# RG-LRU gates of a hybrid layer: two 64-channel blocks on the two halves of the TensorE array's rows

## The chip, the core and the metric

The kernel runs on one core of a Trainium2 chip. The core has five engines that work side by side, each through its own queue in order: PE (TensorE, matmul; its weight loads are shown apart as PEld), DVE (VectorE), ACT (ScalarE), POOL (GpSimd) and SP (SyncE, which issues most transfers). Operands lie in SBUF and matmul results in PSUM, which has eight banks; both memories have 128 partitions, and the partitions of a matmul's operands are the rows of PE's array. The metric is the device time of one execution in microseconds (us).

## The reference

One layer of a streaming encoder: an RMS norm, one combined input projection, differential attention beside a gated linear recurrence (RG-LRU), one output projection and a final norm. The input has 1024 tokens of width 1024, with 16 meta tokens ahead of them (T = 1040). The part that the change concerns is the two gates of the recurrence, each a block-diagonal product with eight blocks of 64 x 64:

```python
def rg_lru(x, w_r, b_r, w_i, b_i, lru_L):
    B, T, C = x.shape                                # C = 512
    xb = x.reshape(B, T, N_LRU_BLOCKS, LRU_BLOCK)    # 8 blocks of 64 channels
    r = jax.nn.sigmoid(jnp.einsum('btnc,ncd->btnd', xb, w_r).reshape(B, T, C) + b_r)
    i = jax.nn.sigmoid(jnp.einsum('btnc,ncd->btnd', xb, w_i).reshape(B, T, C) + b_i)
    log_a = -LRU_C * r * jax.nn.softplus(-lru_L)
    a = jnp.exp(log_a)
    mult = jnp.sqrt(-jnp.expm1(2.0 * log_a))
    mult = mult.at[:, 0].set(1.0)
    b = mult * (i * x)
    ...                                              # h[t] = a[t] * h[t-1] + b[t]
```

## The kernel before

Channels lie on partitions and tokens along the free dimension, so the 512 recurrent channels are four tiles (b = 0 to 3) of 128 partitions x 1040 tokens, two 64-channel blocks in each. A tile's tokens are cut into three thirds of 264, 264 and 512 columns (COLS, line 34), each of which fits a PSUM bank. Every fp32 product is made of three matmuls on a split of its operands into a high and a low part: high x high, high x low, low x high.

**Gates before.** The weights of both gates lie as full 128 x 128 matrices with two 64 x 64 blocks on the diagonal and zeros elsewhere (wg, line 1291; split into wgh and wgl by gate_weights, line 662). For each tile, gate and third, `gate` (line 530) takes one bank, makes three matmuls on all 128 rows, and ACT reads the bank once with a sigmoid on 128 partitions. That is 24 thirds, 72 matmuls and 24 sigmoids.

**Where they run.** The input projection runs in groups of 32 steps by `run_group` (line 685): K, Q, GA (the attention's gate path), GL (the recurrence's gate path), each with four blocks of eight steps over the contraction. A step is six matmuls of 512 columns (in K six of 264 and three of 512). After each step `tick` (line 156) takes items from a background list `bg`, in which conv, split, gates, decay and scan of the four tiles stand in a fixed order (lines 702 to 723). An item has a cost that is charged to a credit, may carry a function that says when its inputs are ready, and an item without a function ends the tick. The times for this come from a model of the engines (`Clock`, line 38) at the time the program is built; what results is one fixed order for each engine. While K runs, the gates of tile 0 use the bank O (`gate_bank`, line 515), later gates use the pool M of three banks, which also serves other work.

**What follows a gate.** On ACT: tanh of gate 0 (named `gate` in the views, by sp4), then `a` (one plus it); DVE then takes five reciprocals of `a` and multiplies gate 1 with xc (`lru_decay`). Then `lru_scan`: a square root on ACT (with a table load ahead), a multiply on DVE, `a` again on ACT, the product with gate 1 and the scan on DVE.

**Beside it on the same two engines.** `split_steps` (line 220) prepares the next group's weights, one contraction step at a time: a copy on ACT (w<-wraw), a subtraction on DVE (w<-wraw,w), and PE needs both in that step of the next group's first block. `qk_evac` (line 617) and `ga_evac` (line 747) take finished blocks out of PSUM: qk on DVE, f16h on ACT, f16l on DVE; for GA a sigmoid gsig on ACT and a product gsig on DVE, two each for a block.

Of the kernel before, what the change touches and what calls it, by code (L numbers as in the profile page):

```python
# [9 lines left out]
F32R = mybir.dt.float32r  # L10
F16 = mybir.dt.float16
BF16 = mybir.dt.bfloat16
AF = mybir.ActivationFunctionType
# [3 lines left out]
P = 128  # L17
NM = 16
S = 1024
T = NM + S  # L20
# [5 lines left out]
NB = 4  # L26
# [72 lines left out]
def hybrid_layer_kernel(ctx: ExitStack, tc: tile.TileContext, xT, x, meta, w6, nwT,  # L99
                        par, wg, lamv, subw, w_out, fnw, cosT, sinT, ident, sel, bmask, out):  # L100
    nc = tc.nc
    clock = Clock()
    V, A, G, PE = (clock.engine(k, e) for k, e in zip(("V", "A", "G", "PE"),
                                                      (nc.vector, nc.scalar, nc.gpsimd, nc.tensor)))
# [14 lines left out]
    def slot(tag, shape, dt=F32, name=None):  # L119
        return big.tile(shape, dt, tag=tag, bufs=BUFS[tag], name=name or tag)  # L120

    def cst(shape, dt=F32, name=None):
        return const.tile(shape, dt, name=name)

    def bank(shape, dt=F32, name="psm"):
        ps = psM.tile(shape, dt, tag="M", name=name)
        clock.ring("M", 3, ps)
        return ps
# [44 lines left out]
    def later(*items):  # L173
        bg.extend(items)
# [140 lines left out]
    for k in range(KC - 2):  # L315
# [3 lines left out]
        if k == 1:  # L319
            pr = cst([P, NB, 8], name="pr")  # L320
# [41 lines left out]
        fetch_w(G_K, k)  # L362


    wgr = slot("V", [P, NB, 2, P], name="wgr")
    dma(wgr, wg)
    cosR = slot("K", [P, T], name="cosR")
    dma(cosR, cosT)
# [14 lines left out]
    def row_of_rstd():  # L383

        dg = slot("raw", [P, 4, P], name="dg"), slot("raw", [P, 4, P], name="dg")
        dm = cst([NM, NM], name="dgm")
        for h in range(2):
            V.tensor_tensor(dg[h], idf.unsqueeze(1).to_broadcast([P, 4, P]),
                            rstd[:, 4 * h:4 * h + 4].unsqueeze(2).to_broadcast([P, 4, P]), op=OP.mult)
        V.tensor_scalar(dm, idf[0:NM, 0:NM], rstd[0:NM, NT:NT + 1], None, op0=OP.mult)  # L390
        yield
        ps, pm = two_banks(), bank([P, NM], name="psx")
        for h in range(2):
            PE.matmul(ps[:, h * 512:(h + 1) * 512], ones, dg[h].rearrange("p t q -> p (t q)"), start=True, stop=True)
            A.copy(Rb[:, NM + h * 512:NM + (h + 1) * 512], ps[:, h * 512:(h + 1) * 512])
        PE.matmul(pm, ones[0:NM, :], dm, start=True, stop=True)
        A.copy(Rb[:, 0:NM], pm)
        yield
# [28 lines left out]
    rows = row_of_rstd()  # L427
# [58 lines left out]
    L = [{} for _ in range(NB)]  # L486
# [26 lines left out]
    in_k = []  # L513

    def gate_bank():
        if in_k:
            ps = psO.tile([P, 512], F32, tag="O", name="psg")
            clock.ring("O", 1, ps)
            return ps
        return bank([P, 512], name="psg")  # L520


    def lru_gates(b):


        def gate_ready(j, h):
            return max(clock.ready(L[b]["ch"], L[b]["cl"]) if j + h == 0 else 0.0,
                       clock.free("O", 1) if in_k else clock.free("M", 3))

        def gate(j, h):  # L530
            ch, cl = L[b]["ch"], L[b]["cl"]
            if h == 0:
                L[b]["ti"[j]] = slot("work", [P, T], name=f"gate{j}")
            r, bias = L[b]["ti"[j]], pr[:, b, 5 + j:6 + j]
            ps = gate_bank()
            s = COLS[h]
            ps = ps[:, 0:s.stop - s.start]
            PE.matmul(ps, wgh[:, b, j, :], ch[:, s], start=True, stop=False)
            PE.matmul(ps, wgh[:, b, j, :], cl[:, s], start=False, stop=False)
            PE.matmul(ps, wgl[:, b, j, :], ch[:, s], start=False, stop=True)  # L540
            A.activation(r[:, s], ps, AF.Sigmoid, bias=bias)

        def tanh():
            t = L[b]["t"]
            A.activation(t, t, AF.Tanh, scale=sp4[:, b:b + 1])
            a = L[b]["a"] = slot("work", [P, T], name="a")
            A.activation(a, t, AF.Identity, bias=1.0)

        for j in range(2):
            for h in range(3):  # L550
                later((0, lambda j=j, h=h: gate(j, h), lambda j=j, h=h: gate_ready(j, h)), (0, None))
        later((0, tanh))

    def lru_decay(b):
# [106 lines left out]

    def gate_weights():
        nonlocal wgh, wgl
        wgh = slot("V", [P, NB, 2, P], F32R, name="wgh")
        wgl = slot("V", [P, NB, 2, P], F32R, name="wgl")
        A.copy(wgh, wgr)
        V.tensor_tensor(wgl, wgr, wgh.bitcast(F32), op=OP.subtract)
        V.tensor_copy(idh, idf)
# [31 lines left out]

    wgh = wgl = None
    later((0, tables), (1.15, gate_weights))
    lru_conv(0)
    lru_split(0)
    lru_conv(1)
    lru_gates(0)
    later((0.6, masks), (0, meta_operand))
    lru_split(1)
    lru_conv(2)
    lru_decay(0)  # L710
    lru_gates(1)
    lru_split(2)
    lru_conv(3)
    later(*lru_scan(0))
    lru_decay(1)
    lru_gates(2)
    lru_split(3)
    later(*lru_scan(1))
# [558 lines left out]
def _layout(i):  # L1277
    f = np.float32
    a = {k: np.asarray(v) for k, v in i.items()}
    x = a["x"][0]  # L1280
    meta = a["meta_tokens"]
    w = a["w_in"][0]

    perm = [m * 64 + half * 8 + j for half in range(2) for m in range(NMAP) for j in range(8)]
    perm += [m * 64 + 16 * b + j for b in range(1, 4) for m in range(NMAP) for j in range(16)]
    perm = np.array(perm)
    cols = [w[:, 2048:2560], w[:, 2560:3072], w[:, 0:512][:, perm], w[:, 512:1024][:, perm],
            w[:, 1536:2048], w[:, 1024:1536]]
    par = np.concatenate([a["conv_w"][0], a["conv_b"], a["b_rgate"], a["b_igate"], a["lru_L"]], 0)
    par = par.reshape(8, NB, P).transpose(2, 1, 0)  # L1290
    wg = np.zeros((P, NB, 2, P), f)
    for n in range(8):
        b, o = n // 2, (n % 2) * 64
        wg[o:o + 64, b, 0, o:o + 64] = a["w_rgate"][0, n]
        wg[o:o + 64, b, 1, o:o + 64] = a["w_igate"][0, n]

    inv = np.power(np.float64(500000.0), -np.arange(0, 16, 2) / 16).astype(f)
    ang = (np.arange(T, dtype=f)[:, None] * inv[None, :]).astype(np.float64)
    row = np.arange(P) % 8
    cosT = np.cos(ang).astype(f).T[row]  # L1300
    sinT = np.sin(ang).astype(f).T[row]
    sinT = np.concatenate([sinT[:64], -sinT[64:]], 0)
    r = np.arange(P)
    sel = (np.arange(32)[:, None] % NM == r[None, :] % NM).astype(f)
    bmask = ((r[:, None] % 64) // NM == np.arange(512)[None, :] // P).astype(f)
    return dict(
        xT=np.concatenate([meta, x], 0).T, x=x, meta=meta,
        w6=np.stack(cols), nwT=a["norm_w"][0].reshape(KC, P).T, par=par, wg=wg,
        lamv=np.concatenate([a["lambda_q1"], a["lambda_q2"], a["lambda_k1"], a["lambda_k2"]], 0),
        subw=a["subln_w"][0].reshape(P, 1), w_out=a["w_out"][0], fnw=a["final_norm_w"],  # L1310
        cosT=cosT, sinT=sinT, ident=np.eye(P, dtype=f), sel=sel, bmask=bmask)
# [19 lines left out]
```

## Time and profile before

| | |
|---|---|
| median of three runs | 486.93 us (486.28 to 487.14) |
| the profiled execution | 486.57 us, of which the profile's span is 484.8 us |
| matmuls of the gates (psg) | 72, from 69.7 to 182.2 us of the span |
| sigmoids of the gates | 24, from 71.0 to 182.4 us |

In rows of the timeline the columns are start and length in us, engine, line, operation, written tile <- read tiles, for PE and PEld the rows * columns of the array that are used, the shape, and the count; in brackets the idle time of the engine ahead of the row and what ended it. In rows for one tile the three numbers are the shortest, median and longest duration in ns, and then the first and last start. In rows of windows come the window, its length, the busy time of PE, PEld, DVE, ACT and POOL with the number of instructions, PE's granted clock, the busy share of the DMA engines and GB/s. All engine operations of this kernel go through one helper and so have its line, L77; one goes by the tiles' names.

### The profile page before, as it was taken

How to read it: one execution, taken by the hardware profiler on the slowest of the kernel's cores; microseconds unless marked ns; L12 is line 12 of the kernel's file. 1: busy time of each engine (PE TensorE's matmuls, PEld its weight loads, DVE VectorE, ACT ScalarE, POOL GpSimd, SP SyncE). 2: the span in 40 equal slices, each digit the busy share in tenths (PEclk: the TensorE clock that was granted, in tenths of full speed). 3: DMA queues.
4: the chain of work that ended last, by engine and by line, in shares of the span. 5: the costliest groups of instructions: out<-in, count | busy, mean ns of one | idle time of the engine just before them, and what ended most of it. 6: DMA issues, size and time to landing. Idle time of an engine off the chain costs nothing.

```text
span 484.8 us, 7748 instructions
## 1 busy us (share of the span) xinstructions
PE 466.2 (96%) x2844; PEld 375.4 (77%) x2844; DVE 364.3 (75%) x610; ACT 303.3 (63%) x592; POOL 126.1 (26%) x171
## 2 busy tenths in 40 slices
PE   6999999999999999999999999999988999999894
PEld 5996989988888888888877577777766778877783
DVE  5756987496799576974574477789999989898443
ACT  5687532663626838441583367698787877797733
POOL 0102202201010000000001044185142425365772
PEclk9999999999999999999999999999999999999998
DMA  7993221344023115239445124953943576315523
GB/s 243 394 398 124 89 89 31 80 121 120 23 65 88 44 43 174 87 124 346 141 139 187 45 61 138 265 172 91 275 110 91 131 193 153 121 32 197 195 88 130
DMA packets 50150, 68.33 MB, mean 141 GB/s; under 512 B 21008, under 2 KB 30128, under 8 KB 50112
## 3 DMA queue, kind: packets, MB, share of 16 engines
q1 hardware_dynamic: 38240, 55.21, 34.6%
q0 software_dynamic: 11872, 12.63, 10.7%
q8 instruction: 22, 0.36, 0.3%
q14 instruction: 16, 0.13, 0.1%
HBM read 48.91 MB, written 18.91 MB: 140 GB/s over the span
## 4 chain that ended last, share of the span: by engine, by line
PE 87%; DVE 5%; ACT 3%; issue 2%; DMA 1%; POOL 0%; POOLq 0%; ACTq 0%; SPq 0%
PE pss L77 42%; PE psv L77 9%; PE psol L77 7%; PE psoa L77 7%; PE ps L77 6%; PE psx L77 5%; PE O L77 4%; DVE e L77 3%; PE psg L77 2%; PE pt L77 2%; DMA res<-res_d 1%; DVE w L77 1%; PE psmr L77 1%; PE pa L77 1%; ACT wT L77 1%
## 5 line engine op out<-in xcount | busy, mean ns | idle before, releaser
L77 PE MATMUL pss<-xs,w 128*128 128x512 f32 (+1 forms) x720 | 142.4, 345 | 4.3 <-ACT xs L77 4.3
L77 PEld LDWEIGHTS pss<-xs,w 128*128 128x128 f32 x720 | 120.4, 190 | 24.5 <-ACT xs L77 4.3
L77 ACT ACTIVATE e<-e,mx 128x528 f32<-128x528 f32 (+7 forms) x64 | 50.5, 790 | 27.4 <-DVE mx L77 26.1
L77 PE MATMUL psv<-w,xs 128*128 128x512 f32 x192 | 48.4, 402 | 0.2 <-DVE v L77 0.2
L77 DVE CUSTOM_DVE_ANT_0 e<-pss,mask,nesc 128x528 f32<-128x528 f32 (+6 forms) x56 | 42.6, 761 | 7.7 <-PE pss L77 6.5
L77 PE MATMUL pss<-w,xs 128*128 128x512 f32 x192 | 46.0, 394 | 0.0
L77 PE MATMUL psol<-woh,lr 128*128 128x512 f32 x128 | 42.8, 415 | 1.9 <-ACT wT L77 1.9
L77 DVE TENSOR_TENSOR w<-wraw,w 128x512 fp32r<-128x512 f32 (+2 forms) x49 | 31.7, 669 | 16.2 <-ACT w L77 16.0
L77 PE MATMUL pss<-kst,qt 128*128 128x512 f16 (+3 forms) x208 | 42.6, 318 | 0.7 <-DVE mx L77 0.7
L77 PEld LDWEIGHTS psv<-w,xs 128*128 128x128 f32 x192 | 35.3, 188 | 10.0 <-issue 0.8
L77 PEld LDWEIGHTS pss<-w,xs 128*128 128x128 f32 x192 | 35.7, 188 | 7.9
L77 PE MATMUL psoa<-woh,at 128*128 128x512 f32 (+1 forms) x136 | 41.6, 389 | 0.2 <-ACT psoa L77 0.2
L77 ACT COPY wT<-pt 128x1024 f16<-128x1024 f16 (+5 forms) x48 | 37.6, 784 | 1.0 <-PE pt L77 0.8
L77 DVE SCALAR_TENSOR_TENSOR e<-e,mx 128x528 f32<-128x528 f32 (+7 forms) x32 | 35.0, 1095 | 1.1
L77 ACT ACTIVATE w<-wraw 128x512 fp32r<-128x512 f32 x47 | 28.5, 619 | 9.7 <-DMA wraw<-in_w_dram 9.2
L77 PE MATMUL ps<-xs,w 128*128 128x512 f32 x120 | 34.4, 394 | 0.0
L77 PEld LDWEIGHTS <-wT 128*128 128x128 f16 x432 | 25.6, 98 | 6.6 <-issue 2.7
L77 PE MATMUL O<-v,wT 128*128 128x128 f16 x432 | 29.4, 219 | 1.3 <-ACT wT L77 1.3
L77 DVE TENSOR_TENSOR w<-e,w 128x528 f16<-128x528 f32 (+7 forms) x32 | 28.9, 904 | 0.9
L77 PEld LDWEIGHTS psol<-woh,lr 128*128 128x128 f32 x128 | 22.9, 188 | 8.6 <-ACT wT L77 3.2
L77 DVE RECIPROCAL a<-a 128x208 f32<-128x208 f32 x20 | 27.8, 1423 | 0.0
L77 PEld LDWEIGHTS psoa<-woh,at 128*128 128x128 f32 x136 | 24.1, 188 | 4.5 <-ACT psoa L77 0.4
(197 smaller groups left out, 838.4 us busy)
## 6 DMA issues: line engine op xcount, KB each, us to landing
wraw<-in_w_dram SPq DMA_DIRECT2D x47, 256.0 KB, 3.9
xt<-in_x_dram SPq DMA_DIRECT2D x8, 512.0 KB, 7.0
woraw<-in_w_out_dram SPq DMA_DIRECT2D x8, 512.0 KB, 3.5
xres<-in_x_dram SPq DMA_DIRECT2D x8, 512.0 KB, 4.9
lr<-lru_d POOLq DMA_DIRECT2D x8, 512.0 KB, 5.1
res_d<-xres SPq DMA_DIRECT2D x8, 512.0 KB, 3.1
res<-res_d SPq DMA_DIRECT2D x8, 512.0 KB, 4.4
out_dram<-res SPq DMA_DIRECT2D x7, 512.0 KB, 2.9
```

The costliest lines, as they stand in the source:

```text
L77: return f(*a, **k)
```

## The change

Both gates of one 64-channel block now lie side by side in one 64 x 128 matrix. The two blocks of a tile have the two halves of the array's rows: rows 0 to 63 for the first, 64 to 127 for the second. The weights shrink to half (128 x 4 x 128). For a tile and a third, `gates` takes two banks, one for each block, and makes three pairs of matmuls on 64 rows each, alternating between the halves. Bank m then holds the gates of block m: for block 0 gate 0 on partitions 0 to 63 and gate 1 on 64 to 127, for block 1 the other way round. Four sigmoids of 64 partitions, two on each bank, carry them to the two gate tiles. There are again 72 matmuls with the same numbers of columns, in 12 groups instead of 24, and 48 sigmoids instead of 24. The list `bg` has three gate items for a tile instead of six, and an item waits for two banks.

```diff
-    wgr = slot("V", [P, NB, 2, P], name="wgr")
+    wgr = slot("V", [P, NB, P], name="wgr")
...
-        def gate_ready(j, h):
-            return max(clock.ready(L[b]["ch"], L[b]["cl"]) if j + h == 0 else 0.0,
-                       clock.free("O", 1) if in_k else clock.free("M", 3))
+        def gate_ready(h):
+            return max(clock.ready(L[b]["ch"], L[b]["cl"]) if h == 0 else 0.0,
+                       max(clock.free("O", 1), clock.free("M", 3)) if in_k else clock.free("M", 2))
 
-        def gate(j, h):
+        def gates(h):
             ch, cl = L[b]["ch"], L[b]["cl"]
             if h == 0:
-                L[b]["ti"[j]] = slot("work", [P, T], name=f"gate{j}")
-            r, bias = L[b]["ti"[j]], pr[:, b, 5 + j:6 + j]
-            ps = gate_bank()
+                for j in range(2):
+                    L[b]["ti"[j]] = slot("work", [P, T], name=f"gate{j}")
             s = COLS[h]
-            ps = ps[:, 0:s.stop - s.start]
-            PE.matmul(ps, wgh[:, b, j, :], ch[:, s], start=True, stop=False)
-            PE.matmul(ps, wgh[:, b, j, :], cl[:, s], start=False, stop=False)
-            PE.matmul(ps, wgl[:, b, j, :], ch[:, s], start=False, stop=True)
-            A.activation(r[:, s], ps, AF.Sigmoid, bias=bias)
+            n = s.stop - s.start
+            banks = gate_bank(), bank([P, 512], name="psg")
+            lohi = slice(0, 64), slice(64, P)
+            for w, x, first, last in ((wgh, ch, True, False), (wgh, cl, False, False), (wgl, ch, False, True)):
+                for m, rows in enumerate(lohi):
+                    PE.matmul(banks[m][:, 0:n], w[rows, b, :], x[rows, s], start=first, stop=last)
+            for m, rows in enumerate(lohi):
+                for c, to in enumerate(lohi):
+                    j = m ^ c
+                    A.activation(L[b]["ti"[j]][rows, s], banks[m][to, 0:n], AF.Sigmoid, bias=pr[rows, b, 5 + j:6 + j])
...
-        for j in range(2):
-            for h in range(3):
-                later((0, lambda j=j, h=h: gate(j, h), lambda j=j, h=h: gate_ready(j, h)), (0, None))
+        for h in range(3):
+            later((0, lambda h=h: gates(h), lambda h=h: gate_ready(h)), (0, None))
...
-        wgh = slot("V", [P, NB, 2, P], F32R, name="wgh")
-        wgl = slot("V", [P, NB, 2, P], F32R, name="wgl")
+        wgh = slot("V", [P, NB, P], F32R, name="wgh")
+        wgl = slot("V", [P, NB, P], F32R, name="wgl")
...
-        wg[o:o + 64, b, 0, o:o + 64] = a["w_rgate"][0, n]
-        wg[o:o + 64, b, 1, o:o + 64] = a["w_igate"][0, n]
+        wg[o:o + 64, b, o:o + 64] = a["w_rgate"][0, n]
+        wg[o:o + 64, b, 64 - o:P - o] = a["w_igate"][0, n]
```

The fixed order of the engines moves with it between 69 and about 212 us of the span; POOL and SP keep their order, and so do all engines in the attention that follows. Three places show it. Numbers that the program gives to buffers differ between the two.

PE, the last gates (tile 3) in the middle of GA, before: pss<-w,xs are GA's matmuls, pss<-xs,w are those of GL.

```order
L77 MATMUL psg<-xch,wgh 128x264
L77 MATMUL psg<-xcl,wgh 128x264
L77 MATMUL psg<-xch,wgl 128x264
L77 MATMUL pss<-w,xs 128x512 x6
L77 MATMUL psg<-xch,wgh 128x512
L77 MATMUL psg<-xcl,wgh 128x512
L77 MATMUL psg<-xch,wgl 128x512
L77 MATMUL pss<-w,xs 128x512 x90
L77 MATMUL pss<-xs,w 128x512 x192
```

The same place now:

```order
L77 MATMUL psg<-xch,wgh 128x264 x2
L77 MATMUL psg<-xcl,wgh 128x264 x2
L77 MATMUL psg<-xch,wgl 128x264 x2
L77 MATMUL pss<-w,xs 128x512 x12
L77 MATMUL psg<-xch,wgh 128x512 x2
L77 MATMUL psg<-xcl,wgh 128x512 x2
L77 MATMUL psg<-xch,wgl 128x512 x2
L77 MATMUL pss<-w,xs 128x512 x78
L77 MATMUL pss<-xs,w 128x512 x192
```

The last gates stand 78 matmuls ahead of GL instead of 90.

ACT, the end of Q, before: f16h are evacuations of Q, w the weights of GA, the gates those of tile 2 (1472 is gate 0, 1515 gate 1).

```order
L77 ACTIVATE f16h<-qk,sc 128x1024
L77 ACTIVATE w<-wraw 128x512 x3
L77 ACT_TABLE_LOAD
L77 ACTIVATE gate_1472<-psg,pr 128x264
L77 ACTIVATE w<-wraw 128x512
L77 ACTIVATE gate_1472<-psg,pr 128x264
L77 ACTIVATE w<-wraw 128x512
L77 ACTIVATE gate_1472<-psg,pr 128x512
L77 ACTIVATE w<-wraw 128x512
L77 ACTIVATE gate_1515<-psg,pr 128x264
L77 ACTIVATE f16h<-qk,sc 128x1024
```

And now (1502 is gate 0, 1503 gate 1):

```order
L77 ACTIVATE f16h<-qk,sc 128x1024
L77 ACTIVATE w<-wraw 128x512 x5
L77 ACT_TABLE_LOAD
L77 ACTIVATE gate_1502<-psg,pr 64x264
L77 ACTIVATE gate_1503<-psg,pr 64x264 x2
L77 ACTIVATE gate_1502<-psg,pr 64x264
L77 ACTIVATE w<-wraw 128x512
L77 ACTIVATE f16h<-qk,sc 128x1024
L77 ACTIVATE gate_1502<-psg,pr 64x264
L77 ACTIVATE gate_1503<-psg,pr 64x264 x2
L77 ACTIVATE gate_1502<-psg,pr 64x264
```

Five weight copies instead of three stand between f16h and the first sigmoid of tile 2. PE's matmuls for the second third of this tile use, on their second bank, the bank that the first two of these sigmoids give back.

DVE, from tile 2's scan to the weights of GL, before: the reciprocals are those of tile 3, w the weights of GL's eight steps, gsig the products of GA, 1675 and 1641 tile 3's gate 1 and gate 0.

```order
L77 SCALAR_TENSOR_TENSOR gate_1515<-a,gate_1472 128x1040
L77 RECIPROCAL a<-a 128x208 x4
L77 TENSOR_TENSOR w<-wraw,w 128x512
L77 RECIPROCAL a<-a 128x208
L77 SCALAR_TENSOR_TENSOR gsig<-pss,rstd,gsig 128x512 x2
L77 TENSOR_TENSOR gate_1675<-gate_1675,xc 128x1040
L77 TENSOR_TENSOR w<-wraw,w 128x512
L77 SCALAR_TENSOR_TENSOR gate_1641<-gate_1641,a 128x1040
L77 TENSOR_TENSOR w<-wraw,w 128x512
L77 TENSOR_TENSOR gate_1641<-gate_1641,gate_1675 128x1039
L77 COPY gate_1641<-gate_1675 128x1
L77 TENSOR_TENSOR w<-wraw,w 128x512 x2
```

And now (1684 and 1683 are tile 3's gate 1 and gate 0):

```order
L77 SCALAR_TENSOR_TENSOR gate_1503<-a,gate_1502 128x1040
L77 RECIPROCAL a<-a 128x208 x3
L77 TENSOR_TENSOR w<-wraw,w 128x512
L77 SCALAR_TENSOR_TENSOR gsig<-pss,rstd,gsig 128x512 x2
L77 RECIPROCAL a<-a 128x208
L77 TENSOR_TENSOR w<-wraw,w 128x512
L77 RECIPROCAL a<-a 128x208
L77 TENSOR_TENSOR w<-wraw,w 128x512
L77 TENSOR_TENSOR gate_1684<-gate_1684,xc 128x1040
L77 TENSOR_TENSOR w<-wraw,w 128x512 x2
L77 SCALAR_TENSOR_TENSOR gate_1683<-gate_1683,a 128x1040
L77 TENSOR_TENSOR w<-wraw,w 128x512 x2
```

Two reciprocals that stood ahead of the product gsig of GA's third block now stand behind it, between the weights of GL's first three steps; tile 3's scan (gate 1 from `a` and gate 0) moves from between the weights of steps 4 and 5 to behind the last of them.

More of the change, by code (lines that the diff above doesn't have):

```diff
@@ L1290, in _layout @@
     par = par.reshape(8, NB, P).transpose(2, 1, 0)
-    wg = np.zeros((P, NB, 2, P), f)
+    wg = np.zeros((P, NB, P), f)
     for n in range(8):
         b, o = n // 2, (n % 2) * 64
-        wg[o:o + 64, b, 0, o:o + 64] = a["w_rgate"][0, n]
-        wg[o:o + 64, b, 1, o:o + 64] = a["w_igate"][0, n]
+        wg[o:o + 64, b, o:o + 64] = a["w_rgate"][0, n]
+        wg[o:o + 64, b, 64 - o:P - o] = a["w_igate"][0, n]
     inv = np.power(np.float64(500000.0), -np.arange(0, 16, 2) / 16).astype(f)
```

## The prediction

> **What bounds the kernel now.** First the page: spans, engines and the chain that ended last.
>
> ```profile
> span 484.8 us, 7748 instructions
> PE 466.2 (96%) x2844; PEld 375.4 (77%) x2844; DVE 364.3 (75%) x610; ACT 303.3 (63%) x592; POOL 126.1 (26%) x171
> PE 87%; DVE 5%; ACT 3%; issue 2%; DMA 1%; POOL 0%; POOLq 0%; ACTq 0%; SPq 0%
> ```
>
> Then the view by windows for the stages in which gates run (K from 57, Q from 105.5, the gate-path projection GA from 154.6, GL from 203), and the row of the gate weights' copy.
>
> ```profile
> 57.00:68.00 11.00, 11.00 (x71) 9.96 (x70) 10.31 (x13) 4.13 (x8) 0.00 (x0) 1.00 0.34 122
> 68.00:183.00 115.00, 115.00 (x591) 97.63 (x591) 89.65 (x95) 62.22 (x90) 15.20 (x38) 1.00 0.24 65
> 183.00:248.00 65.00, 65.00 (x285) 52.48 (x284) 44.30 (x50) 34.21 (x52) 3.31 (x6) 1.00 0.58 185
> L77 ACT CAST wgh<-wgr x1: 1034/1034/1034, 58.4 to 58.4; 128x1024 fp32r<-128x1024 f32 x1
> ```
>
> PE (the number after the length) is never idle there; PEld, DVE and ACT follow. So what PE gains or loses between 57 and 248 us goes straight to the end, and the other engines count only where PE comes to wait for them. The halved gate weights (half of a 1.03 us copy on ACT, half of a subtraction on DVE, half of one transfer) lie beside this full PE; I cost them at nothing, and without that cover they would be worth half a microsecond.
>
> **The matmuls.** The timeline of PE shows the pace.
>
> ```profile
> 112.45 0.28 PE L77 MATMUL psg<-xch,wgh 128*128 128x264 f32 x1
> ...
> 112.81 1.55 PE L77 MATMUL pss<-xs,w 128*128 128x512 f32 x6
> ...
> 115.94 0.39 PE L77 MATMUL psg<-xch,wgh 128*128 128x512 f32 x1
> ...
> 116.63 1.55 PE L77 MATMUL pss<-xs,w 128*128 128x512 f32 x6
> ```
>
> Three gate matmuls of 264 columns take 112.81 - 112.45 = 0.36 us, 0.12 each; three of 512 take 0.69, 0.23 each. Before, one third of one tile costs six: 0.72 or 1.38 us. There are eight such groups of 264 and four of 512. After, a group is three pairs, one matmul on rows 0-63 and one on rows 64-127, into different banks. No row of this trace shows two halves side by side: a pair costs between one matmul (0.12, 0.23) and two. I take one, because the two share neither array rows nor a bank, so neither has to wait for what the other holds; I keep two for the range. The Trainium skill ("TensorEngine Tiling (Array Packing)", Key Properties) says that different tiles load weights and multiply in parallel; no run here shows it yet.
>
> **The switches.** Going from full-height matmuls to fewer rows and back is shown, with 16 and 32 rows.
>
> ```profile
> 45.71 0.59 PE L77 MATMUL pss<-dg,ones 128*128 128x512 f32 x1
> 46.23 0.29 PEld L77 LDWEIGHTS psx<-dgm,ones 16*128 16x128 f32 x2 [0.76 <-DVE sp L77]
> 277.78 0.18 PEld L77 LDWEIGHTS psvm<-mrows,sl 32*128 32x128 f32 x1
> 277.78 0.29 PEld L77 LDWEIGHTS psvm<-mrows,sl 32*128 32x128 f32 x2
> 278.31 0.59 PE L77 MATMUL psvm<-mrows,sl 32*128 32x512 f32 x1
> 278.83 0.53 PEld L77 LDWEIGHTS psv<-w,xs 128*128 128x128 f32 x3 [0.76 <-issue]
> ```
>
> Two loads follow each other by 0.29 - 0.18 = 0.11. So the first psvm matmul streams from 277.89, and the second from 278.31: a stream takes 0.42. The second ends at 278.73, but the full-height load behind it, which otherwise runs under the matmul ahead, starts only at 278.83. A switch back thus costs 0.10 of waiting and 0.11 of uncovered load, some 0.20 us. The way in is the same: 45.71 + 0.42 = 46.13, load at 46.23. Each of the twelve groups switches twice, 0.40 us. Bounds for 64 rows: a load alone (0.11) and this 0.20; I take 0.20, the measured one.
>
> Sum on PE: a group of 264 becomes 0.40 + 0.36 = 0.76 instead of 0.72, a group of 512 becomes 0.40 + 0.69 = 1.09 instead of 1.38. 8 x 0.04 - 4 x 0.29 = **-0.8 us**. The switches eat nearly all of the halving.
>
> **The sigmoids.** The same columns are read twice, 64 partitions at a time, with 48 instructions for 24.
>
> ```profile
> L77 ACT ACTIVATE gate<-psg,pr x24: 462/482/692, 71.0 to 182.4; 128x264 f32<-128x264 f32 x16, 128x512 f32<-128x512 f32 x8
> L77 DVE TENSOR_TENSOR ropet<-ps,sinR x2: 674/680/686, 76.6 to 78.0; 64x512 f32<-64x512 f32 x2
> ```
>
> No ACT row has 64 partitions; half the time and all of it are the bounds, and I take all of it: durations here go with columns, and DVE's ropet piece of 64x512 takes 0.68 us, like the last 128x512 row quoted below (0.67). Back to back they start 0.1 closer than their length: 0.38 and 0.59. ACT gains 13 us of work over 115 us. Mostly that is hidden, as ACT is busy for 62 of those 115 us. Two places look late, by the changed order of ACT and DVE.
>
> First, the end of Q.
>
> ```profile
> 122.65 0.69 ACT L77 ACTIVATE gate<-psg,pr 128x512 f32<-128x512 f32 x1 [1.61 <-PE psg L77]
> 128.68 3.98 DVE L77 SCALAR_TENSOR_TENSOR xc<-XL,pr,xc 128x1039 f32<-128x1039 f32 x3 [0.96 <-ACT xc L77]
> ...
> 140.80 4.07 DVE L77 RECIPROCAL a<-a 128x208 f32<-128x208 f32 x3
> ...
> 147.23 1.21 DVE L77 TENSOR_TENSOR qk<-pss,Rb 128x1024 f32<-128x1024 f32 x1
> 148.54 1.15 ACT L77 ACTIVATE f16h<-qk,sc 128x1024 f16<-128x1024 f32 x1 [8.17 <-DVE qk L77]
> 149.60 1.66 ACT L77 ACTIVATE w<-wraw 128x512 fp32r<-128x512 f32 x3
> 151.27 1.28 ACT L77 ACT_TABLE_LOAD   x1
> 152.21 0.39 PE L77 MATMUL psg<-xch,wgh 128*128 128x512 f32 x1
> ```
>
> DVE runs without a pause from 128.68 to 148.4, and f16h waits for its qk. The run begins when ACT's xc is done, behind tile 1's last sigmoid at 122.65. That third now ends 0.7 later on PE and has four sigmoids (3 x 0.59 more): 2.5 us later; one reciprocal moves behind qk (1.3 back). So f16h starts near 149.8, five weight copies follow instead of three (2 x 0.52), the table load ends at 154.9, and the first bank is free two sigmoids later, at 155.8. PE wants it for tile 2's second third: the first starts at 151.1 (its place at 152.21 before, less two gate groups of 0.36 and 0.4 saved earlier), plus 0.76, twelve matmuls of 0.23, and the switch: 154.8. **+1.0 us**; everything behind the waiting matmul in PE's queue stands too. Bounds: 0 if f16h isn't late, 1.1 if it is later.
>
> Second, the weights of GL. Queued behind tile 3's last third on ACT and DVE:
>
> ```profile
> 182.22 21.02 PE L77 MATMUL pss<-w,xs 128*128 128x512 f32 x90
> 203.07 12.17 PE L77 MATMUL pss<-xs,w 128*128 128x512 f32 x52
> 187.78 1.24 DVE L77 SCALAR_TENSOR_TENSOR gate<-gate,a 128x1040 f32<-128x1040 f32 x1 [4.36 <-ACT gate L77]
> 192.70 5.36 DVE L77 RECIPROCAL a<-a 128x208 f32<-128x208 f32 x4
> 197.98 0.63 DVE L77 TENSOR_TENSOR w<-wraw,w 128x512 fp32r<-128x512 f32 x1
> 199.88 1.31 DVE L77 SCALAR_TENSOR_TENSOR gsig<-pss,rstd,gsig 128x512 f32<-128x512 f32 x2
> 201.11 1.23 DVE L77 TENSOR_TENSOR gate<-gate,xc 128x1040 f32<-128x1040 f32 x1
> 210.96 0.67 DVE L77 TENSOR_TENSOR w<-wraw,w 128x512 fp32r<-128x512 f32 x1
> ```
>
> Count from the end s of the last gate stream. Before: s = 182.22, GL 20.85 later, the eight weight subtractions (w) from 16.4 to 29.4. GL's step k, 1.39 us each, needs its w 0.46 into the step, the last at 20.85 + 9.73 + 0.46 = 31.0: in time. After: only 78 matmuls stand between, so GL starts at 0.2 + 78 x 0.232 = 18.3. DVE's multiply starts 1.8 later (three more sigmoids of 0.59), at 7.3; then as before 4.9 to the reciprocals, three of 1.32, w, the two gsig (1.23), and now reciprocal, w, reciprocal, w, product with xc, w, w: w of steps 1, 2, 3 end at about 20.0, 21.9 and 23.7. PE needs them at 20.1, 21.5 and 22.9: it waits 0.4 twice. The last stands behind tile 3's multiply and, through two weight copies that ACT now makes only after that, ends near 30.2 by the same durations; PE needs it at 18.3 + 9.7 + 0.5 + 0.8 = 29.3: 0.9 more. Rounded, **+1.7 us**; bounds 0 and 2.5, as half a microsecond on DVE per wait decides.
>
> Sum: -0.8 + 1.0 + 1.7 = **+1.9 us** against the profiled execution's own 486.57, that is 488.4; the median of the runs shown, 486.93, is 0.36 above that execution, so 488.8 for a median. A measurement of this kernel can tell about 0.2% (1 us) from no change.
>
> **Rivals.** (A) ACT and DVE keep up, and both waits fall away: 486.93 - 0.8 = 486.1, not slower. For it: the two estimates are differences of long queues, ACT idles 8.17 us ahead of f16h, and sigmoids on 64 partitions may be shorter. It decides if the w of step 2 lands 0.4 us sooner and the table load 1.0 sooner. If a switch also costs a load alone, 24 x 0.09 = 2.2 us go as well: 483.9. (B) Pairs take longer than one matmul because their loads queue up, 0.11 apart as in psvm's rows. A group of 264 is then 0.10 + 6 x 0.107 + 0.12 + 0.20 = 1.06, of 512 0.10 + 2 x 0.107 + 0.69 + 0.20 = 1.20: 8 x 0.34 - 4 x 0.18 = +2.0, 2.8 above my sum: 491.6. Against it: loads of different rows need not share a path. The Trainium skill ("TensorE: Matmul & The Clock Gate", Measured speedup vs the span model) gives 3.07 times for four row tiles of 512 columns, no row here shows it; a pair at 4/3.07 = 1.30 matmuls would make the groups +0.8 instead of -0.8, an estimate of 490.4. (C) The halves do not overlap: each group only pays its switches, 12 x 0.40 = +4.8, with the waits 494.4. Nothing in this trace excludes it.
>
> **Numbers.** Forecast 0.45 (of it 0.08 within 0.2%), A 0.20 (half faster, half the same), B 0.20, C 0.15. Faster 0.10, same 0.18, slower 0.72. The range from 485.5 to 492.0 holds the forecast, B and most of A, and leaves out C.
>
> **What would show it.** Pairs: gate matmuls that start together, a group 0.4 us beyond three streams; B shows loads 0.11 apart inside a group, C starts a full matmul apart. Switches: PEld idle at both ends of each group. Waits: PE idle for ACT near 155 us, and for DVE w in GL's first block; PE full there means A. I am wrong if a switch at 64 rows costs nothing, or if PE waits at a place not named here.

## The result, and the profile after

The changed kernel takes 491.40 us (median of 4 runs, 491.29 to 491.41), the kernel before 486.67 beside it (486.28 to 487.14): a ratio of 1.0096, 95% interval 1.0079 to 1.0114. That is 4.7 us slower; forecast were 1.9. The profiled execution of the changed kernel took 491.4 with a span of 489.6. Its page, spans, engines and the chain that ended last:

```profile
span 489.6 us, 7782 instructions
PE 467.0 (95%) x2844; PEld 369.1 (75%) x2844; DVE 363.4 (74%) x610; ACT 317.4 (65%) x616; POOL 126.0 (26%) x171
PE 71%; DVE 9%; ACT 9%; DMA 5%; issue 4%; SPq 1%; POOL 0%; POOLq 0%; DVEq 0%; ACTq 0%
```

ACT has 14.1 us more work (317.4 for 303.3). PE's share of the chain falls from 87 to 71%, and DVE and ACT together rise from 8 to 18%: PE now waits for them. The view by windows says where (length, then PE, PEld, DVE, ACT, POOL, each with its instructions):

```profile
57.00:68.00 11.00, 11.00 (x72) 9.96 (x71) 9.87 (x13) 4.46 (x9) 0.00 (x0) 1.00 0.38 134
68.00:183.00 115.00, 112.76 (x583) 91.12 (x582) 80.84 (x88) 71.27 (x106) 15.22 (x38) 1.00 0.23 65
183.00:248.00 65.00, 63.43 (x271) 49.32 (x271) 49.10 (x52) 34.45 (x48) 2.66 (x5) 1.00 0.49 163
```

PE was full in all three windows before. Now it stands for 115 - 112.76 = 2.2 us in the second and 1.6 in the third. Nothing is lost behind 248 us: there the matmuls run 4.8 late, and they still do at the end.

**The gate groups** came out as forecast. PE's timeline around one third of 264 columns:

```profile
112.41 1.32 PE L77 MATMUL pss<-xs,w 128*128 128x512 f32 x5
113.66 0.39 PE L77 MATMUL psg<-xch,wgh 64*128 64x264 f32 x2
113.88 0.29 PE L77 MATMUL psg<-xcl,wgh 64*128 64x264 f32 x2
114.00 0.28 PE L77 MATMUL psg<-xch,wgl 64*128 64x264 f32 x2
114.22 2.35 PE L77 MATMUL pss<-xs,w 128*128 128x512 f32 x9
```

Each row holds a pair of two halves, and the rows follow each other as single matmuls do (114.00 - 113.88 = 0.12). Without the switch in, the first pair would have started at 112.41 + 5 x 0.232 = 113.57, so the group takes 114.22 - 113.57 = 0.65 and leaves another 0.10 of load uncovered behind it: 0.75, forecast 0.76. A group of 512 takes 1.08 (185.73 to 186.62 below, and 0.1 at either end), forecast 1.09. Against the 0.72 and 1.38 of before the twelve groups gain 4 x 0.30 - 8 x 0.03 = 1.0 us. The Trainium skill ("TensorEngine Tiling (Array Packing)", Key Properties) says that different tiles load weights and multiply in parallel; here the trace agrees, with two loads and two matmuls in each row's time.

**The waits** are what went wrong. ACT's timeline, then PE's, at the end of Q:

```profile
123.34 2.77 ACT L77 ACTIVATE gate<-psg,pr 64x512 f32<-64x512 f32 x4 [0.51 <-PE psg L77]
127.00 1.15 ACT L77 ACTIVATE f16h<-qk,sc 128x1024 f16<-128x1024 f32 x1 [0.89 <-DVE qk L77]
...
131.16 1.25 ACT L77 ACTIVATE xc<-XL,pr 128x1040 f32<-128x1040 f32 x1
...
150.78 1.15 ACT L77 ACTIVATE f16h<-qk,sc 128x1024 f16<-128x1024 f32 x1 [7.83 <-DVE qk L77]
151.84 2.70 ACT L77 ACTIVATE w<-wraw 128x512 fp32r<-128x512 f32 x5
154.55 1.28 ACT L77 ACT_TABLE_LOAD   x1
155.85 1.96 ACT L77 ACTIVATE gate<-psg,pr 64x264 f32<-64x264 f32 x4
```

```profile
153.19 1.55 PE L77 MATMUL pss<-w,xs 128*128 128x512 f32 x6
154.67 0.39 PE L77 MATMUL psg<-xch,wgh 64*128 64x264 f32 x1
156.87 0.39 PE L77 MATMUL psg<-xch,wgh 64*128 64x264 f32 x1 [1.82 <-ACT gate L77]
...
157.43 1.88 PE L77 MATMUL pss<-w,xs 128*128 128x512 f32 x7
```

The two halves of a pair, which start together in the group above (one row of x2), stand 156.87 - 154.67 = 2.20 apart, and the whole group takes 157.43 - 154.67 = 2.76 for 114.22 - 113.66 = 0.56: a wait of **2.2 us** for the second bank, which two of the sigmoids from 155.85 on have to free. Then PE's timeline from GA on, and DVE's products with gsig:

```profile
179.90 0.28 PE L77 MATMUL psg<-xch,wgl 64*128 64x264 f32 x2
180.60 1.66 PE L77 MATMUL pss<-w,xs 128*128 128x512 f32 x6 [0.43 <-DVE gsig L77]
...
186.62 18.40 PE L77 MATMUL pss<-w,xs 128*128 128x512 f32 x78
205.30 3.49 PE L77 MATMUL pss<-xs,w 128*128 128x512 f32 x14 [0.28 <-DVE gsig L77]
209.01 7.60 PE L77 MATMUL pss<-xs,w 128*128 128x512 f32 x30 [0.23 <-DVE w L77]
217.24 1.20 PE L77 MATMUL pss<-xs,w 128*128 128x512 f32 x4 [0.62 <-DVE w L77]
218.78 5.57 PE L77 MATMUL pss<-xs,w 128*128 128x512 f32 x23 [0.34 <-DVE gsig L77]
```

```profile
179.14 1.41 DVE L77 SCALAR_TENSOR_TENSOR gsig<-pss,rstd,gsig 128x512 f32<-128x512 f32 x2 [2.47 <-ACT gsig L77]
...
203.75 1.40 DVE L77 SCALAR_TENSOR_TENSOR gsig<-pss,rstd,gsig 128x512 f32<-128x512 f32 x2
...
217.31 1.41 DVE L77 SCALAR_TENSOR_TENSOR gsig<-pss,rstd,gsig 128x512 f32<-128x512 f32 x2
```

Three blocks start when the second product of an earlier block has ended (180.55, 205.15, 218.72) and with it the buffer pss is free. How long each wait is, is read from starts, since the ends of matmuls are modelled. At 180.60: 0.70 behind the last pair, where 0.22 is usual (114.00 to 114.22), so 0.5. At 205.30: 18.68 behind 186.62; without a wait the same 78 matmuls take 18.24 (183.98 to 202.22 in the last run of "Do the waits add up?"), so 0.4. From 205.30 to 218.78 there are 14 + 30 + 4 = 48 matmuls in 13.48 for 48 x 0.232 = 11.1: 2.3 us, of which w takes 0.4, 0.3 (inside the row of 30) and 0.8, gsig at 218.78 0.5, and the loads that no matmul covered after a wait 0.1 each, with one more behind 218.78. **All waits: 2.2 + 0.5 + 0.4 + 2.3 + 0.1 = 5.5 us; less 1.0 of the groups, 4.5 of the 4.7 measured.**

### The profile page after: what moved, and what is told of

Same layout as the page of the kernel before. It is cut to its first block, busy times and chain, and to the rows that moved or that the text cites. A ratio compares the mean times of both kernels' runs of the same rounds, so it can differ in the third digit from the quotient of the medians.

```text
span 489.6 us, 7782 instructions
## 1 busy us (share of the span) xinstructions
PE 467.0 (95%) x2844; PEld 369.1 (75%) x2844; DVE 363.4 (74%) x610; ACT 317.4 (65%) x616; POOL 126.0 (26%) x171
## 4 chain that ended last, share of the span: by engine, by line
PE 71%; DVE 9%; ACT 9%; DMA 5%; issue 4%; SPq 1%; POOL 0%; POOLq 0%; DVEq 0%; ACTq 0%
PE pss L77 30%; PE psv L77 9%; PE psol L77 7%; PE psoa L77 7%; PE ps L77 6%; PE O L77 4%; DVE e L77 3%; ACT gate L77 2%; PE pt L77 2%; PE psx L77 2%; PE psg L77 2%; DMA xt<-in_x_dram 2%; DMA wraw<-in_w_dram 1%; DVE w L77 1%; ACT L77 1%
## 5 line engine op out<-in xcount | busy, mean ns | idle before, releaser
L77 PE MATMUL pss<-xs,w 128*128 128x512 f32 (+1 forms) x720 | 144.2, 347 | 6.1 <-ACT xs L77 4.3
L77 ACT ACTIVATE gate<-psg,pr 64x264 f32<-64x264 f32 (+1 forms) x48 | 26.2, 546 | 10.5 <-PE psg L77 9.9
```

Source lines behind the costliest of these rows:

```text
L77: return f(*a, **k)
```

## The experiments

Theory W: the waits come from ACT's 24 extra sigmoids. Rival O: they come from the new order (three groups of four sigmoids for six of one, two banks at once, other places in the queues). Each run stands against the kernel before on the same chip, 486.6 to 487.0 there. Profiled executions differ by up to 1.5 us in the stretch ahead of 46 us, which no edit touches, so tenths are read between two places of one trace.

**Work or order.** Three kernels, each with the queues of its parent word for word apart from the edit. Order kept, sigmoids over 128 partitions again:

```
-  A.activation(L[b]["ti"[m ^ c]][rows, s], banks[m][to, 0:n], ...)      # four
+  nc.scalar.activation(L[b]["ti"[m]][:, s], banks[m][:, 0:n], ...)      # two
```

> The changed kernel with its order kept, but one sigmoid over 128 partitions for each bank (24 in all, as before) in place of two over 64 (48). The two halves of the input gate's rows and of the other gate's rows come out exchanged for part of the rows, so the gates' values are not the reference's; nothing else is left out. Theory W (the 13 us of extra sigmoids push ACT's and DVE's queues, and the some 5 us of waits of PE come from that work): the waits near 157, 180, 205 and 209 to 219 us go, and what stays is the gain of the gate groups, 486.7 - 0.8 = 485.9, at most 487. Theory O (the waits come from the new order: three groups in place of six, two banks at once, other places in the queues): they stay, 490 to 491.4.

Measured: 487.24, ratio 1.0016 (1.0006 to 1.0026). Some 4.1 of the 4.7 us go with the work, but W's 485.9 is missed. Two waits are left in PE's timeline, both in GL's first block:

```profile
202.79 9.87 PE L77 MATMUL pss<-xs,w 128*128 128x512 f32 x42
213.15 1.19 PE L77 MATMUL pss<-xs,w 128*128 128x512 f32 x4 [0.48 <-DVE w L77]
214.69 5.56 PE L77 MATMUL pss<-xs,w 128*128 128x512 f32 x23 [0.35 <-DVE gsig L77]
```

Together 214.69 - 202.79 - 46 x 0.232 = 1.2 us. With 24 sigmoids as before, they come with the new order, in which 78 matmuls stand between the last gate group and GL for 90; no run moves that place alone. Up to GL no wait is left, and there the gain of the groups shows by itself: from the step of K that PE starts at 46.81 to the start of GL it takes 202.34 - 46.81 = 155.5 us, for 203.07 - 46.55 = 156.5 from the same step in the kernel before. The other side, the kernel before with each sigmoid in two halves:

```
-  A.activation(r[:, s], ps, AF.Sigmoid, bias=bias)
+  for o in (slice(0, 64), slice(64, P)):
+      nc.scalar.activation(r[o, s], ps[o], AF.Sigmoid, bias=pr[o, b, 5 + j:6 + j])
```

> The kernel before, with its order and its matmuls, but each of the 24 sigmoids made as two over 64 partitions. Only ACT's work grows, by some 13 us. W: most of the waits appear here too, 489.5 to 491.5. O: ACT hides them, 486.7 to 487.2.

Measured: 488.80, ratio 1.0049 (1.0037 to 1.0061), between the two theories. Its losses are small and elsewhere: against the trace of before, PE falls back 0.6 us near 72 and 0.3 near 76 (for ACT's sigmoids), 0.4 from 154 to 158 and 0.6 from 210 on (for w), together 1.9. Work alone costs 2.2, order alone 0.6 with the groups' gain in it, both 4.7: together they cost more than their sum. That each eats the slack which hid the other is my reading; no run isolates it. Then the matmuls over the full height, with order, banks and sigmoids of the changed kernel:

```
-  for m, rows in enumerate(lohi): PE.matmul(banks[m][:, 0:n], w[rows, b, :], x[rows, s], ...)
+  for m in range(2): PE.matmul(banks[m][:, 0:n], w[:, b, m, :], x[:, s], ...)
```

> The changed kernel with its order, its two banks and its 48 sigmoids, but the gate matmuls over the full height again (block-diagonal weights, six per third), so that there are no halves and no switches. The waits stay under W and under O. If the halves and switches cost what the prediction says (8 thirds at 0.76 for 0.72, 4 at 1.09 for 1.38), this is up to 0.8 slower than the changed kernel, less where the later matmuls find ACT and DVE further on: 491.4 to 492.2. If instead the halves or the switches cost PE more than their groups show (theory P), this is clearly faster than the changed kernel: 489 or less.

Measured: 492.18, ratio 1.0114 (1.0101 to 1.0127), 0.8 above the changed kernel, with waits at the same seven places. The two intervals touch, so the 0.8 is rough, but it is near the 1.0 that the rows of the groups show, and theory P, 489 or less, falls.

**Does a pair need its order?** The loops over the halves and over the three products are exchanged:

```
+  for m, rows in enumerate(lohi):
       for w, x, first, last in ((wgh, ch, True, False), ...):
-          for m, rows in enumerate(lohi):
               PE.matmul(banks[m][:, 0:n], w[rows, b, :], x[rows, s], ...)
```

> The changed kernel, but the three matmuls of rows 0-63 come first in PE's queue and the three of rows 64-127 behind them, instead of in pairs. If halves overlap only where neighbours in the queue use different rows, one pair in three still overlaps: a third of 264 is then five matmuls long plus its switches (0.60 + 0.40 = 1.00 for 0.76), one of 512 1.15 + 0.40 = 1.55 for 1.09: 8 x 0.24 + 4 x 0.46 = 3.8 more on PE, of which the waits may take up to 2: 493 to 495. If the order in the queue does not matter, it stays at 491.4.

Measured: 493.01 in the median, but in two clusters: 490.7 and 491.2 at a granted clock of 0.998, 493.0 to 494.0 at 0.994. The profiled one is the 490.7; what slowed the others wasn't profiled and stays open. PE's timeline of that run, whose queue has three matmuls of rows 0-63 and then three of rows 64-127:

```profile
113.02 0.40 PE L77 MATMUL psg<-xch,wgh 64*128 64x264 f32 x2
113.25 0.29 PE L77 MATMUL psg<-xcl,wgh 64*128 64x264 f32 x2
113.37 0.29 PE L77 MATMUL psg<-xch,wgl 64*128 64x264 f32 x2
113.59 1.20 PE L77 MATMUL pss<-xs,w 128*128 128x512 f32 x4
```

The pairs are there all the same, and the group takes no longer: 113.59 - 113.02 = 0.57, for 114.22 - 113.66 = 0.56. My 3.8 us were wrong; the second half's matmuls do not stand behind the first half's. PE thus does not keep strictly to its queue here: the first matmul of rows 64-127 starts in the row of 113.02, ahead of the second and third of rows 0-63 that stand before it.

**Do the waits add up?** Each cure takes one kind of wait away and leaves the 48 sigmoids. Tile 2's second third, 12 matmuls later in PE's queue:

```
-  clock.free("M", 2))
+  clock.free("M", 2) + (2.0 if (b, h) == (2, 1) else 0.0))
```

> The changed kernel, but tile 2's second third stands 12 matmuls (2.8 us) later in PE's queue, behind the point at which its bank comes free; nothing else moves on any engine. If the waits of PE add up, the 2.1 us near 157 go: 489.3. If the wait there only gave ACT and DVE time that PE takes back later, the waits near 180 and in GL grow by as much: 491.4.

Measured: 489.82, ratio 1.0053 (1.0040 to 1.0067), 1.6 below the changed kernel. The wait of 2.2 is gone, and the six later ones stand as they were (0.3 to 0.8 each): PE's standing there gave nobody time that these needed. But the gain is smaller than the wait. Tile 2's next group, of 512 columns, now waits 0.4 for its own second bank; the rows are shown with the last cure below. GL's low weights off DVE:

```
-  V.tensor_tensor(w[:, 1, :], r, w[:, 0, :].bitcast(F32), op=OP.subtract)
+  nc.gpsimd.tensor_tensor(w[:, 1, :], ...)      # for G_GL alone
```

> The changed kernel with its order, but the eight subtractions that make GL's low weights (w) run on GpSimd instead of DVE. If GL's waits come from DVE's queue, the three for w (0.39, 0.26, 0.79) and the two for gsig (0.44, 0.50) go, with the load of 0.1 that each of the five leaves uncovered: 491.4 - 2.9 = 488.5. If gsig is late by ACT, only those for w go: 489.7. If GpSimd is too slow (some 1.3 us each) or PE then waits elsewhere: 491.

Measured: 488.67 in the median of 488.62 to 490.55, ratio 1.0047 (1.0030 to 1.0064), 2.7 below. All five waits of GL are gone; DVE's queue was their cause, for gsig too. Both edits:

> The changed kernel with both edits: the third 12 matmuls later, GL's subtractions on GpSimd. If all waits add up, 491.4 - 2.1 - 2.9 = 486.4, and only the wait near 180 (0.5) stays; if each cure moves its wait, 488.5 to 490.

Measured: 486.91, ratio 0.9998 (0.9989 to 1.0008). By the idle time that the timeline lists, one wait is left, for gsig at 178.6. So gsig goes ahead of tile 1's square root, whose table load it had to wait for:

```
-  return [(0, root), (1.2, mult), ...
+  return [(0, root, lambda: 0.0 if seen or b != 1 else 1e9), (1.2, mult), ...   # seen: gsig issued
```

> The changed kernel with both cures, and the two sigmoids of GA's first block (gsig) and their two products ahead of tile 1's square root instead of behind it, on ACT and DVE; nothing else moves. The last wait of PE in the gate stages (0.55 at 179 us, for gsig) goes: 486.9 - 0.55 = 486.3, which is the kernel before less the 0.8 of the gate groups, within a few tenths. If the square root, now 1.4 later, makes tile 1's and tile 3's chains late, a new wait stands in GA or GL: 486.9 or more.

Measured: 486.75, ratio 0.9995 (0.9985 to 1.0006); 486.3 lies inside that interval, and so does no gain at all. The windows and the start of GL in PE's timeline:

```profile
57.00:68.00 11.00, 11.00 (x72) 9.92 (x70) 9.74 (x14) 4.29 (x9) 0.00 (x0) 1.00 0.38 117
68.00:182.00 114.00, 114.00 (x588) 92.20 (x588) 84.33 (x90) 72.06 (x107) 15.17 (x38) 1.00 0.24 65
182.00:248.00 66.00, 66.00 (x289) 52.73 (x289) 44.55 (x48) 38.75 (x59) 15.27 (x14) 1.00 0.58 184
```

```profile
183.98 18.40 PE L77 MATMUL pss<-w,xs 128*128 128x512 f32 x78
202.22 22.13 PE L77 MATMUL pss<-xs,w 128*128 128x512 f32 x95
```

By the windows PE is full again with all 48 sigmoids in place. They hide one wait, of a single half while the other half's matmul still runs, in this run as in the two others with the later third. PE's timeline at tile 2's group of 512:

```profile
162.05 0.85 PE L77 MATMUL psg<-xch,wgh 64*128 64x512 f32 x2
...
163.30 0.97 PE L77 MATMUL pss<-w,xs 128*128 128x512 f32 x3
```

It takes 163.30 - 162.05 = 1.25 for 186.62 - 185.73 = 0.89, 0.4 more. GL starts at 202.22 for 203.07 before; 0.2 of this lies ahead of 46 us already, and the rest, 0.65, is the groups' gain of 1.0 less this wait. So extra work on ACT costs nothing by itself, only where it makes PE wait.

**A version that beats both?** Pairs only where they pay, at the thirds of 512:

```
   for j in range(2):
-      for h in range(3): later((0, gate(j, h), ...))
+      for h in range(2): later((0, gate(j, h), ...))
+  later((0, pair, pair_ready), (0, None))
```

> The kernel before, with pairs only for the third of 512 columns of each tile (block-diagonal matmuls and one sigmoid per gate stay for the thirds of 264; the pairs' weights are copied together by GpSimd). PE gains 4 x 0.29 = 1.2, ACT's extra sigmoids are 8 x 0.59 = 4.7 us instead of 13. If the waits stay away at this amount of work: 485.5. If they grow with the work in proportion (4 us of waits for 13 us of work, as the run with wide sigmoids showed): 485.5 + 1.5 = 487.

Measured: 491.21, ratio 1.0086 (1.0071 to 1.0100). Both guesses missed: a third of the extra sigmoids, and as much loss as with all. 1.4 us of it come from my own copies on GpSimd. POOL's and DVE's timelines:

```profile
64.14 2.18 POOL L77 CAST wp<-wgl 64x512 fp32r<-64x512 f32 x2 [2.95 <-DVE wgl L77]
```

```profile
64.13 4.61 DVE L77 SCALAR_TENSOR_TENSOR xc<-XL,pr,xc 128x1039 f32<-128x1039 f32 x3
```

These three take 3.97 us in the kernel before, and two subtractions beside the earlier pair of copies take 0.98 and 1.10 for 0.68; the first gate group hangs on them. Then PE waits 1.1 at 156, 1.2 at 205.8 and 1.3 at 212, for the same three reasons as above. Transfers in place of these copies made it worse:

```
-  G.tensor_copy(wp[o, m]..., g[o, :, :, o]...)                              # at 59 to 66 us
+  nc.gpsimd.dma_start(wp[o, m, :, j * 64:j * 64 + 64], g[o, :, j, o])       # behind the first groups
```

> The run pairs_at_512 again, but the pairs' weights are copied together by four pairs of small transfers, issued after the first gate groups, and no longer by GpSimd, whose four copies lay beside DVE operations that took up to 1.7 in place of 1.3 us and made the first gate group 1.4 us late. If that was the cause of the 1.4 us, 491.2 - 1.4 = 489.8, with the other waits (1.1 at 156, 1.2 at 206, 1.3 at 212) as they were. If it was the order, 491.2.

Measured: 496.67, ratio 1.0205 (1.0188 to 1.0221). The first group is on time now, but the first pair waits over 4 us for the transfers, the last of which was issued only at 87.9. Behind that, PE's granted clock is 0.70 from 90.5 to 96 (the rows are in the last section): another 5.5 x 0.30 = 1.7 us. The two cures on top:

> The same with GL's subtractions on GpSimd: the waits at 206 and 212 (2.5, with 0.2 of loads) go, 487.1.

> The same, and tile 2's fourth gate group stands 6 matmuls (1.4 us) later in PE's queue: the wait of 1.1 at 156 goes as well, 486.0. All waits gone it would be 486.9 - 4 x 0.29 = 485.8, the first version under the kernel before by more than can be measured.

Measured: 499.02 and 496.76 (1.0255 and 1.0207). The wait at 156 goes in the second of them; the wait for w does not, it becomes 2.5 us for GpSimd. The clock costs more here, too: it is 0.57 and 0.58 from 87 to 95, some 3.4 us each, and in the first of the two 0.66 from 217 to 222, 1.7 more. What worked in one order failed in another, and a part of that is the clock. No version that is measurably faster than the kernel before was found.

## Why the prediction was right in kind and too small

- **The groups** (-0.8): right in every term, -1.0 in the sum, since 0.01 less on each of twelve groups adds up. Pairs run side by side, switches take 0.19 each way. Rivals B and C, which priced loads in a queue, pairs of 1.30 matmuls and halves that don't overlap, fall by PE's timeline; A falls by the waits.
- **The halved weights** at nothing: right, no wait of PE lies near them.
- **The wait at the end of Q** (+1.0): right place and cause, 2.2 in size, twice its own upper bound of 1.1, for which no row was given. The step that failed is "So f16h starts near 149.8": it started at 150.78. I let xc come 2.5 us later behind tile 1's last sigmoid. It came at 131.16 for 127.41, 3.75 later: the sigmoids took 0.4 longer than I had it, and an f16h of Q, which stood behind `a` and xch, now stands directly behind the sigmoids, where ACT waits 0.89 for DVE's qk. Behind a late f16h everything follows to the tenth: five copies, the table load to 155.83, two sigmoids, 156.8.
- **The waits in GL's first block** (+1.7 for w of steps 2, 3 and 7, at 0.4, 0.4 and 0.9): those three came at 0.4, 0.3 and 0.8. What failed is that I priced only w. The two gsig products ahead of w in the same queue also free the buffer of PE's next block; by my own count they ended just in time, and they ended late (0.4 and 0.5 in GL, 0.5 in GA). And each wait costs another 0.1, because the load behind it isn't covered.
- **"I take all of it"** for a sigmoid over 64 partitions: right for its length, wrong for its room. "Back to back they start 0.1 closer than their length: 0.38 and 0.59" holds for 128 partitions only. Four over 64 take 1.96 and 2.77, 0.49 and 0.69 each: some 0.1 more per sigmoid, 0.4 per third, on margins that were smaller than that.

Forecast -0.8 + 1.0 + 1.7; measured -1.0 + 2.2 + 2.8 (GL) + 0.5 (GA). The cures show that these terms are real and, but for the 0.4 that comes back in tile 2's next group, separate. The chains to the waits were worked out with errors of up to 1.0 us, and a queue near its limit turns each of these into time of PE.

## What to carry to other kernels

When a change adds work to an engine that is off the critical path, list every instruction by which the critical engine depends on it (buffers that it frees as well as operands that it makes), with the margin of each; a margin under your error of estimate may turn out a wait, and such waits add up. Here a saving of 1.0 us did not pay for 24 more instructions on an engine whose queue PE waits in, and with the places in that queue set again it came out even. Test a suspected wait by moving one instruction: if the others stay as they were, the waits are separate, and each can be cured by itself. Look for small new waits by the starts, too: a view of busy time hides a wait of one half of the array.

## What the runs showed of the hardware that was not expected

- Row halves overlapped in both orders tried in PE's queue: three matmuls on rows 0-63 and then three on rows 64-127 ran as three pairs, in 0.57 us, like the alternating ones in 0.56.
- Sigmoids over 64 partitions did not overlap their neighbours, those over 128 did by 0.1 us: 2.77 for four of 512 columns, while ahead of the change a sigmoid of 0.69 that began at 182.42 had the next instruction start at 183.00.
- Where the small transfers stopped and started PE several times within a few microseconds, it went on at about half speed. In the run pairs_at_512_by_dma, the view by windows (the last three numbers are PE's granted clock, the DMA share and GB/s) and PE's timeline:

```profile
86.00:90.50 4.50, 1.95 (x6) 0.84 (x6) 1.85 (x3) 0.68 (x1) 4.50 (x9) 0.99 0.94 114
90.50:96.00 5.50, 5.50 (x26) 4.81 (x26) 0.00 (x0) 5.04 (x6) 2.63 (x17) 0.70 0.50 132
96.00:104.00 8.00, 8.00 (x52) 7.22 (x51) 7.71 (x8) 3.80 (x8) 0.00 (x0) 1.00 0.11 32
```

```profile
92.24 1.48 PE L77 MATMUL ps<-xs,w 128*128 128x512 f32 x3
93.52 1.02 PE L77 MATMUL pss<-xs,w 128*128 128x264 f32 x6
```

Three matmuls of 512 columns take 93.52 - 92.24 = 1.28, 0.43 each for 0.23. PE had been busy for 1.95 of the 4.5 us before, with no stop longer than 1.9; the clock was back within 5.5. The Trainium skill ("TensorE: Matmul & The Clock Gate", Part 1: The HAM clock gate) says that the array falls to half its clock after an idle window of some 3.4 us, and returns after a busy one. The trace agrees on the half and on the few microseconds; but PE was only mostly idle here, never for 3.4 us at a stretch. What decides is open: in the two runs built on this one a later wait of 2.4 us (for w from GpSimd, near 216) was followed by a clock of 0.66 in the one and of 1.00 in the other, both from 217 to 222. The waits of the changed kernel, 2.2 us and less, each by itself, cost no clock (1.00 in its three windows).
